# First modulation: silu(c) as the weight and the modulation matrix moving, in four column quarters

## The chip, the core and the metric

The kernel runs on one NeuronCore of a Trainium2 chip. Its engines are TensorE (PE, with its weight loads listed as PEld), VectorE (DVE), ScalarE (ACT), GpSimd (POOL) and SyncE (SP), which issues the DMAs. The metric is the device time of one execution in microseconds, the median of the runs.

## The reference, cut to what matters

Two transformer blocks of two layers each are computed for 512 tokens of width 1024, all in float32. Each layer of the first block scales and shifts its normalised input by vectors that depend on a condition `c`:

```python
def adaln_params(c, w, b):
    m = jax.nn.silu(c) @ w + b
    return [t[:, None, :] for t in jnp.split(m, 6, axis=-1)]
...
        sh1, sc1, g1, sh2, sc2, g2 = adaln_params(c, ada_w[layer], ada_b[layer])
        h = rms_norm(x, norm_mix_g[layer]) * (1.0 + sc1) + sh1
        if layer % 2 == 0:
            xr, gr, q, k, v = jnp.split(h @ ev_w_in[e], N_EVEN_SPLITS, axis=-1)
```

The change concerns `sh1` and `sc1` of layer 0: 2 x 1024 numbers, each a sum over 1024 products, needed before the first projection can start.

## The kernel before

Features lie on the 128 partitions, so a 1024-wide vector is 8 chunks of 128, and activations are stored as chunks of 128 x 512 tokens. Projections run three float32r matmuls for each product (high x high, high x low, low x high parts), 512 columns each in the startup.

The startup is `layer0_in`. It spawns eight tasks `first_chunk(c)`. Each loads 1 MB of the modulation matrix (two tiles `raw` of 128 x 4 x 256 floats: for 8 k chunks the 128 columns of the shift and the 128 of the scale that belong to chunk c), multiplies it with `silu_c`, adds the bias on DVE (tile `mod`), makes the scale column (`A`), and from that the chunk of h: `t` on DVE, the high part on ACT, the low part on DVE. Beside them `first_w(k)` loads a strip of 128 x 768 projection weights, whose high part ACT casts and whose low part DVE forms. `xnorm_all` sums squares of x, has PE spread the sum over the partitions by the matrix `ones`, and forms `rstd` on ACT and DVE. The main task then runs, for each of the 8 chunks k, six banks of three matmuls: 144 matmuls of 128x512, that end in six PSUM banks. ACT copies these out, and the attention and recurrence of layer 0 begin.

All engines execute their own queue in order. The order is fixed when the program is built: `Flow` runs the tasks with estimated costs, and each engine takes the ready operation of the best priority. A changed cost or a new operation can therefore move other operations. The other modulation vectors (layer 0 segments 2 to 5 and layer 1) are made in the background by DVE (`ada_half`: one step for each k chunk, 140 steps of the form `t<-a,silu_c,t`), folded into the tile `adap`, and turned by small PE matmuls against `sel`.

In `first_chunk` before, a 128x128 block of the matrix is the weight and one column of `silu_c` moves: 16 matmuls for a chunk, each with one output column. A float32 matmul appears in the trace as two records. PE's matmuls are all written in a helper, so they share line 304.

Of the kernel before, what the change touches and what calls it, by code (L numbers as in the profile page):

```python
# [13 lines left out]
ALU = mybir.AluOpType  # L14
AX = mybir.AxisListType

P = 128
S = 512
D = 1024
KC = 8  # L20
# [36 lines left out]
LAT = 0.15  # L57
# [33 lines left out]
class Flow:  # L91
# [18 lines left out]
    def put(s, name, n=1):  # L110
        s.free[name] += n
        still = []
        for t, k, spare in s.waiting[name]:
            if s.free[name] >= k + spare:
                s.free[name] -= k
                s.at(s.now, s.step, t, None)
            else:
                still.append((t, k, spare))
        s.waiting[name] = still
# [89 lines left out]
def body(ctx, tc, I, out, upto=8):  # L209
    nc = tc.nc  # L210
    T, V, A, G = nc.tensor, nc.vector, nc.scalar, nc.gpsimd
# [11 lines left out]
    ev, spawn, put = fl.event, fl.spawn, fl.put  # L223
# [4 lines left out]
    def mk(pool, shape, dt=F32, tag=None):  # L228
        cnt[0] += 1
        return pools[pool].tile(list(shape), dt, tag=tag or pool, name=f"{pool}{cnt[0]}", bufs=BUFS.get(tag))  # L230

    def big(dt=F32, shape=(P, 2, S)):
        return mk("a", shape, dt)

    def tmp(n=S):
        return mk("t", (P, n))
# [4 lines left out]
    def bank():  # L241
        cnt[0] += 1
        return psp.tile([P, S], F32, tag="b", name=f"b{cnt[0]}")

    def const(name, shape, dt=F32):
        return cp.tile(list(shape), dt, tag=name, name=name)


    def size(ap):
        n = 1  # L250
        for d in ap.shape[1:]:
            n *= d
        return n

    def ve(n, fast=False):
        return (0.52 if fast else 1.04) * n * 1e-3 + 0.07
# [4 lines left out]
    def tt(o, a, b, op, prio=None):  # L261
        return Op("V", ve(size(o)), lambda: V.tensor_tensor(o, a, b, op), prio=prio)  # L262

    def stt(o, a, sc, b, op0, op1, prio=None):
        return Op("V", ve(size(o)) + ptr(sc), lambda: V.scalar_tensor_tensor(o, a, sc, b, op0, op1), prio=prio)  # L265
# [6 lines left out]
    def vcopy(o, a, fast=True):  # L272
        return Op("V", ve(size(o), fast), lambda: V.tensor_copy(o, a))  # L273
# [11 lines left out]
    def act(o, a, f, bias=None, scale=1.0, accum=None, prio=None):  # L285
        kw = {}
        if bias is not None:
            kw["bias"] = bias
        if accum is not None:
            kw["accum_out"] = accum  # L290
        c = 0.83e-3 * size(o) + 0.07 + 0.09 * (not isinstance(scale, float)) + 0.09 * (accum is not None) + 0.12 * (bias is not None)
        return Op("A", c, lambda: A.activation(o, a, f, scale=scale, **kw), tab=SET_OF.get(f.name), prio=prio)  # L292

    def acopy(o, a):
        return Op("A", 0.83e-3 * size(o) + 0.07, lambda: A.copy(o, a))  # L295
# [4 lines left out]
    def mm(cost, *args, lat=0.0):  # L300

        def go():
            for o, l, r, st, sp in args:
                T.matmul(o, l, r, start=st, stop=sp)  # L304
        return Op("T", cost, go, lat=lat)
# [11 lines left out]
    def f4(n):  # L317

        return n / 600 + 0.0133
# [8 lines left out]
    vec = const("vec", (P, NVEC))  # L328
# [8 lines left out]
    sel4 = const("sel4", (P, 4, P))  # L337
    eps = const("eps", (P, 1))
    silu_c = const("silu_c", (P, 8))
    adap = const("adap", (P, 192))  # L340
    mods = [const(f"mod{l}", (P, 48)) for l in range(2)]
    acol = {k: const("A%d%d" % k, (P, 8)) for k in ((0, 1), (0, 4), (1, 1), (1, 4))}

    def vv(name, j=None):
        o, w = VEC[name]
        return vec[:, o : o + w] if j is None else vec[:, o + j : o + j + 1]
# [598 lines left out]
    def setup():  # L945
        G.memset(ones, 1.0 / D)
        G.memset(eps, EPS)
        yield Op("D", 0.3, lambda: nc.sync.dma_start(vec, I["vec"]), lat=2.2)
        yield act(silu_c, vv("c"), AF.Silu)

    const_done, decay_done = ev(), []

# [47 lines left out]
    def first_chunk(c, x, ready, nd, loaded):  # L1000

        raw = [big(shape=(P, 4, 256)) for _ in range(2)]
        yield [Op("D", 1.45, lambda i=i: nc.sync.dma_start(raw[i], I["ada0"][c, i]), lat=2.2) for i in range(2)]
        loaded.set()
        yield ready
        yield ("pt", 1)
        ps = bank()
        yield mm(16 * 0.111, *[(ps[:, i : i + 1], raw[k // 4][:, k % 4, i * P : i * P + P], silu_c[:, k : k + 1], k == 0, k == KC - 1)
                               for i in range(2) for k in range(KC)], lat=LAT)
        put("a", 2)  # L1010
        sh, sc = mods[0][:, c : c + 1], mods[0][:, 8 + c : 9 + c]
        o = VEC["ada_b0"][0]
        yield [tt(sh, ps[:, 0:1], vec[:, o + c : o + c + 1], ALU.add), tt(sc, ps[:, 1:2], vec[:, o + 8 + c : o + 9 + c], ALU.add)]
        put("pt")
        a = acol[0, 1][:, c : c + 1]
        yield stt(a, sc, 1.0, vv("gm0", c), ALU.add, ALU.mult)
        yield ("t", 1)
        t = tmp()
        for e in nd:
            yield e  # L1020
        yield stt(t, xs[c], a, rstd, ALU.mult, ALU.mult)
        yield act(x.h(c), t, AF.Identity, bias=sh)
        yield stt(x.l(c), t, sh, x.h(c).bitcast(F32), ALU.add, ALU.subtract)
        put("t")
        for hf in range(2):
            x.ready[c][hf].set()
# [9 lines left out]
    def layer0_in():  # L1036
# [3 lines left out]
        def after(e, gen):  # L1040
            yield e
            yield from gen

        ready = spawn(setup(), P_CRIT)

        def load_x(i):
# [15 lines left out]
        def chunks():  # L1062
            prev = []
            for c in range(KC):
                yield ("a", 2)
                prev.append(spawn(first_chunk(c, x, ready, nd, loaded[c]), P_CRIT))
                yield ("fw", 1)
                yield ("a", 3)
                fw[c] = (big(F32R, (P, 768)), big(F32R, (P, 768)))
                spawn(first_w(c, fw[c], fr[c]), P_CRIT)  # L1070
            yield loaded[CC]
            spawn(consts(), P_CRIT)
            yield loaded[KC - 1]
            spawn(weights(), P_W)
            for d in prev:
                yield d
# [931 lines left out]
```

## Time and profile before

| | us |
|---|---|
| median of 3 runs | 2870.63 |
| lowest, highest | 2869.69, 2872.17 |
| the profiled execution | 2870.89 |
| its span in the trace | 2869.1 |
| PE busy in it | 2789.7 (97%) |
| DVE busy | 1809.6 (63%) |
| ACT busy | 1257.5 (44%) |

Times of a view count from the start of the span; 1.8 us of the execution lie outside it. A busy PE is not a PE at its peak: the granted clock and the kind of matmul say what a busy microsecond does. In the views of the trace, the time in square brackets at the end of a row is the idle time of the engine ahead of it and what ended it.

### The profile page before, as it was taken

How to read it: one execution, taken by the hardware profiler on the slowest of the kernel's cores; microseconds unless marked ns; L12 is line 12 of the kernel's file. 1: busy time of each engine (PE TensorE's matmuls, PEld its weight loads, DVE VectorE, ACT ScalarE, POOL GpSimd, SP SyncE). 2: the span in 40 equal slices, each digit the busy share in tenths (PEclk: the TensorE clock that was granted, in tenths of full speed). 3: DMA queues.
4: the chain of work that ended last, by engine and by line, in shares of the span. 5: the costliest groups of instructions: out<-in, count | busy, mean ns of one | idle time of the engine just before them, and what ended most of it. 6: DMA issues, size and time to landing. Idle time of an engine off the chain costs nothing.

```text
span 2869.1 us, 44005 instructions
## 1 busy us (share of the span) xinstructions
PE 2789.7 (97%) x17374; PEld 2483.8 (87%) x17374; DVE 1809.6 (63%) x4137; ACT 1257.5 (44%) x2733; POOL 5.0 (0%) x54
## 2 busy tenths in 40 slices
PE   8998999999999999999989999989999999899999
PEld 7886987888988888898979888889899999788888
DVE  3798997447677444588794333666766767853333
ACT  2674432324654322256553322455655554442221
POOL 0000000000000000000000000000000000000000
PEclk8998999999999999999999999999999999999999
DMA  6444366232122232321222223221121122213321
GB/s 249 142 159 172 118 207 218 88 103 74 60 67 82 88 105 93 105 88 45 68 88 74 93 99 103 97 66 62 58 71 66 56 75 89 74 60 103 102 97 66
DMA packets 80271, 281.91 MB, mean 98 GB/s; under 512 B 8896, under 2 KB 11712, under 8 KB 80064
## 3 DMA queue, kind: packets, MB, share of 16 engines
q1 hardware_dynamic: 80064, 279.10, 28.6%
q8 instruction: 136, 2.23, 0.3%
q14 instruction: 71, 0.58, 0.1%
HBM read 276.97 MB, written 2.10 MB: 97 GB/s over the span
## 4 chain that ended last, share of the span: by engine, by line
PE 90%; DVE 6%; issue 1%; ACT 1%; DMA 1%; SPq 0%; DVEq 0%; ACTq 0%
PE b L304 86%; PE b L310 4%; DVE t L262 1%; DVE t L265 1%; DVE a L262 1%; DMA a<-in_ada_dram 1%; DVE x L262 1%; DVE x L265 1%; DVE a L265 0%; ACT t L292 0%; ACT a L295 0%; DVE a L1141 0%; ACT a L292 0%; DVE s L276 0%; DVE s L262 0%
## 5 line engine op out<-in xcount | busy, mean ns | idle before, releaser
L304 PE MATMUL b<-a,a 128*128 128x256 f32 (+4 forms) x15024 | 2560.3, 333 | 21.3 <-DVE a L262 8.1
L304 PEld LDWEIGHTS b<-a,a 128*128 128x128 f32 (+1 forms) x15024 | 2211.5, 191 | 294.5 <-issue 24.3
L295 ACT CAST a<-a 128x1024 fp32r<-128x1024 f32 (+1 forms) x354 | 357.4, 1034 | 319.8 <-DVE a L262 199.7
L262 DVE TENSOR_TENSOR a<-a,a 128x1024 fp32r<-128x1024 f32 (+2 forms) x362 | 428.4, 1195 | 8.3 <-ACT a L295 6.3
L292 ACT ACTIVATE t<-b 128x512 f32<-128x512 f32 x150 | 88.8, 597 | 345.6 <-PE b L304 344.6
L262 DVE TENSOR_TENSOR x<-b,x 128x512 f32<-128x512 f32 (+1 forms) x144 | 81.5, 571 | 206.6 <-PE b L304 206.1
L295 ACT COPY t<-b 128x512 f32<-128x512 f32 (+3 forms) x186 | 98.0, 529 | 195.8 <-PE b L304 123.9
L265 DVE SCALAR_TENSOR_TENSOR x<-b,mod,x 128x256 f32<-128x256 f32 (+1 forms) x176 | 104.7, 602 | 111.7 <-PE b L304 110.6
L295 ACT COPY a<-b 128x512 f32<-128x512 f32 (+2 forms) x178 | 85.1, 480 | 180.8 <-PE b L304 116.9
L273 DVE CAST a<-t 128x512 fp32r<-128x512 f32 x64 | 27.3, 426 | 203.6 <-ACT t L292 203.6
L265 DVE SCALAR_TENSOR_TENSOR a<-a,vec,a 128x256 fp32r<-128x256 f32 x288 | 132.4, 479 | 34.8 <-ACT a L292 34.2
L310 PE MATMUL b<-ident,t 128*128 128x128 f32 x832 | 131.1, 280 | 19.5 <-DVE t L262 12.0
L304 PEld LDWEIGHTS b<-a,t 128*128 128x128 f32 x1024 | 128.6, 197 | 12.4 <-ACT t L295 4.5
L304 PE MATMUL b<-a,t 128*128 128x64 f32 (+1 forms) x1024 | 135.2, 279 | 2.4 <-ACT t L295 2.3
L292 ACT ACTIVATE a<-a,vec 128x256 fp32r<-128x256 f32 x288 | 132.3, 500 | 1.0 <-DMA a<-in_kvw_dram 0.9
L310 PEld LDWEIGHTS b<-ident,t 128*128 128x128 f32 x832 | 97.9, 144 | 37.3 <-DVE t L262 15.1
L292 ACT ACTIVATE t<-t,s,s 128x256 f32<-128x256 f32 (+3 forms) x192 | 113.4, 593 | 23.4 <-DVE s L265 23.2
L292 ACT ACTIVATE t<-t 128x512 f32<-128x512 f32 x108 | 67.6, 633 | 122.9 <-DVE t L265 121.1
L262 DVE TENSOR_TENSOR t<-t,t 128x256 f32<-128x256 f32 (+5 forms) x201 | 104.6, 523 | 18.2 <-ACT t L292 16.9
L262 DVE TENSOR_TENSOR a<-t,a 128x512 fp32r<-128x512 f32 (+1 forms) x188 | 107.6, 596 | 4.0 <-ACT a L295 0.7
L276 DVE TENSOR_REDUCE s<-t 128x8 f32<-128x512 f32 (+1 forms) x84 | 56.4, 672 | 80.8 <-ACT t L292 80.6
L265 DVE SCALAR_TENSOR_TENSOR t<-a,silu_c,t 128x512 f32<-128x512 f32 x140 | 104.4, 746 | 1.4
(101 smaller groups left out, 1461.7 us busy)
## 6 DMA issues: line engine op xcount, KB each, us to landing
a<-in_ada_dram SPq DMA_DIRECT2D x96, 512.0 KB, 4.5
a<-in_gu_dram SPq DMA_DIRECT2D x88, 512.0 KB, 4.3
a<-in_mu_dram SPq DMA_DIRECT2D x64, 512.0 KB, 4.1
a<-in_md_dram SPq DMA_DIRECT2D x64, 512.0 KB, 3.7
a<-in_kvw_dram SPq DMA_DIRECT2D x48, 512.0 KB, 4.1
a<-in_dn_dram SPq DMA_DIRECT2D x44, 512.0 KB, 3.8
a<-in_aqkv_dram SPq DMA_DIRECT2D x24, 512.0 KB, 4.2
a<-in_bwq_dram SPq DMA_DIRECT2D x24, 512.0 KB, 3.7
```

Of the source, the lines that this page charges most:

```text
L262: return Op("V", ve(size(o)), lambda: V.tensor_tensor(o, a, b, op), prio=prio)
L265: return Op("V", ve(size(o)) + ptr(sc), lambda: V.scalar_tensor_tensor(o, a, sc, b, op0, op1), prio=prio)
L273: return Op("V", ve(size(o), fast), lambda: V.tensor_copy(o, a))
L276: return Op("V", ve(size(a)), lambda: V.tensor_reduce(o, a, AX.X, ALU.add))
L292: return Op("A", c, lambda: A.activation(o, a, f, scale=scale, **kw), tab=SET_OF.get(f.name), prio=prio)
L295: return Op("A", 0.83e-3 * size(o) + 0.07, lambda: A.copy(o, a))
L304: T.matmul(o, l, r, start=st, stop=sp)
L310: T.transpose(o, a, ident)
```

## The change

`silu(c)` becomes the weight. It is stored as `silu32`, 8 blocks of 128x32 of which only the first column is not zero. For each k chunk, 256 columns of the matrix (128 of the shift, 128 of the scale) move through a 32-column quarter of the array, quarter k % 4, into partitions 32 (k % 4) and following of a bank; two k chunks share a quarter and accumulate. The eight matmuls leave four partial sums in rows 0, 32, 64 and 96, and zeros in the other rows. ACT copies the 128x256 block to SBUF, and two matmuls with a column of ones (`one1`) sum over the partitions and turn the rows into the two columns that DVE reads as before.

```diff
+    silu32 = const("silu32", (P, 8, 32))
+    one1 = const("one1", (P, 1))
...
+        G.memset(one1, 1.0)
+        G.memset(silu32, 0.0)
...
+        yield vcopy(silu32[:, :, 0:1], silu_c.unsqueeze(2))
...
         ps = bank()
-        yield mm(16 * 0.111, *[(ps[:, i : i + 1], raw[k // 4][:, k % 4, i * P : i * P + P], silu_c[:, k : k + 1], k == 0, k == KC - 1)
-                               for i in range(2) for k in range(KC)], lat=LAT)
+        part = lambda i: ps[i * 32 : i * 32 + 32, :256]
+
+        yield mm(4 * f4(256) / 2 + 0.1, *[(part(k % 4), silu32[:, k, :], raw[k // 4][:, k % 4, :], k < 4, k > 3) for k in range(KC)], lat=LAT)
         put("a", 2)
+        yield ("t", 1)
+        rows = tmp(256)
+        yield acopy(rows, ps[:, :256])
+        yield mm(2 * 0.222, *[(ps[:, 256 + i : 257 + i], rows[:, i * P : i * P + P], one1, True, True) for i in range(2)], lat=LAT)
+        put("t")
...
-        yield [tt(sh, ps[:, 0:1], vec[:, o + c : o + c + 1], ALU.add), tt(sc, ps[:, 1:2], vec[:, o + 8 + c : o + 9 + c], ALU.add)]
+        yield [tt(sh, ps[:, 256:257], vec[:, o + c : o + c + 1], ALU.add), tt(sc, ps[:, 257:258], vec[:, o + 8 + c : o + 9 + c], ALU.add)]
```

On PE, from the norm's matmul (`t,ones`) to the first projection matmuls (`a,a 128x512`), the order before is this; `silu_c` marks the modulation's one-column matmuls of chunks 1 and 2:

```order
L304 MATMUL b_200<-t_120,ones 128x512
L304 MATMUL b_224<-silu_c,a_132 128x1 x4
L304 MATMUL b_224<-silu_c,a_133 128x1 x4
L304 MATMUL b_224<-silu_c,a_132 128x1 x4
L304 MATMUL b_224<-silu_c,a_133 128x1 x4
L304 MATMUL b_262<-silu_c,a_135 128x1 x4
L304 MATMUL b_262<-silu_c,a_136 128x1 x4
L304 MATMUL b_262<-silu_c,a_135 128x1 x4
L304 MATMUL b_262<-silu_c,a_136 128x1 x4
L304 MATMUL b_111<-a_103,a_123 128x512
```

The same place on PE after the change; `32x256` are the quarter matmuls, `one` the turning ones, and tile numbers differ between the two programs:

```order
L304 MATMUL b_197<-t_124,ones 128x512
L304 MATMUL b_186<-one_89,t_203 128x1 x2
L304 MATMUL b_227<-a_136,silu_88 32x256 x4
L304 MATMUL b_227<-a_137,silu_88 32x256 x4
L304 MATMUL b_227<-one_89,t_241 128x1 x2
L304 MATMUL b_257<-a_139,silu_88 32x256 x4
L304 MATMUL b_257<-a_140,silu_88 32x256 x4
L304 MATMUL b_113<-a_105,a_127 128x512
L304 MATMUL b_113<-a_106,a_127 128x512
L304 MATMUL b_113<-a_105,a_128 128x512
L304 MATMUL b_114<-a_105,a_127 128x512
L304 MATMUL b_114<-a_106,a_127 128x512
```

Sixteen rows of one column become eight of 256, and the two turning matmuls of a chunk stand behind other work: chunk 0's behind the norm's matmul, chunk 2's behind six projection matmuls.

On ACT before, between the cast of the first weight strip and the first two chunks of h:

```order
L295 CAST a_123<-a_131 128x768
L292 ACTIVATE t_121<-b_200,eps 128x512
L292 ACTIVATE rstd<-t_121 128x512
L292 ACTIVATE t_121<-rstd 128x512
L295 CAST a_125<-a_134 128x768
L292 ACTIVATE a_103<-t_218,mod_89 128x512
```

On ACT after, the same place, where each COPY of 128x256 is a new operation that waits for the quarter matmuls of its chunk:

```order
L295 CAST a_127<-a_135 128x768
L295 COPY t_203<-b_186 128x256
L292 ACTIVATE t_125<-b_197,eps 128x512
L292 ACTIVATE rstd<-t_125 128x512
L292 ACTIVATE t_125<-rstd 128x512
L295 CAST a_129<-a_138 128x768
L295 COPY t_241<-b_227 128x256
L292 ACTIVATE a_105<-t_222,mod_91 128x512
```

The copy of chunk 0 has moved in ahead of the norm's first operation, and that of chunk 1 ahead of the first chunk of h.

## Rows read from the trace of the kernel before

**Rows 1.** The page, part 4: shares of the chain that ended last.
```profile
PE 90%; DVE 6%; issue 1%; ACT 1%; DMA 1%; SPq 0%; DVEq 0%; ACTq 0%
```
**Rows 2.** Timeline of PE, 0 to 98 us: start, us, engine, line, operation, xcount.
```profile
11.94 6.96 PE L304 MATMUL b<-silu_c,a 128*128 128x1 f32 x32 [11.94 <-DMA a<-in_ada_dram]
18.76 2.06 PE L304 MATMUL b<-t,ones 128*128 128x512 f32 x2
20.61 13.65 PE L304 MATMUL b<-silu_c,a 128*128 128x1 f32 x64
34.12 4.00 PE L304 MATMUL b<-a,a 128*128 128x512 f32 x9
37.95 3.90 PE L304 MATMUL b<-silu_c,a 128*128 128x1 f32 x32
...
52.00 4.25 PE L304 MATMUL b<-silu_c,a 128*128 128x1 f32 x32
...
60.11 6.82 PE L304 MATMUL b<-silu_c,a 128*128 128x1 f32 x32
...
81.04 3.63 PE L304 MATMUL b<-silu_c,a 128*128 128x1 f32 x32
84.53 25.72 PE L304 MATMUL b<-a,a 128*128 128x512 f32 x143
```
**Rows 3.** Windows of PE: stretch, its length, PE busy (records), PEclk, DMA share, GB/s.
```profile
10.00:20.00 10.00, 8.06 (x34) 1.00 1.03 416
...
38.00:54.00 16.00, 16.00 (x91) 0.89 0.34 108
54.00:72.00 18.00, 18.00 (x69) 0.53 0.47 153
72.00:84.00 12.00, 12.00 (x85) 1.00 0.28 95
...
480.00:500.00 20.00, 20.00 (x90) 1.00 0.32 106
```
**Rows 4.** Timeline of DVE in the startup: the norm's sum, its last steps.
```profile
13.05 0.69 DVE L262 TENSOR_TENSOR t<-t,t 128x512 f32<-128x512 f32 x1
...
23.68 0.43 DVE L270 TENSOR_SCALAR t<-t 128x512 f32<-128x512 f32 x1
27.47 0.23 DVE L262 TENSOR_TENSOR mod<-b,vec 128x1 f32<-128x1 f32 x2 [3.36 <-PE b L304]
...
28.48 0.69 DVE L262 TENSOR_TENSOR rstd<-rstd,t 128x512 f32<-128x512 f32 x1
```
**Rows 5.** Timeline of ACT: a weight cast, the norm's first step, the first bank copy.
```profile
14.04 0.83 ACT L295 CAST a<-a 128x768 fp32r<-128x768 f32 x1 [1.22 <-DMA a<-in_evfirst_dram]
...
20.91 0.69 ACT L292 ACTIVATE t<-b,eps 128x512 f32<-128x512 f32 x1 [6.05 <-PE b L304]
...
94.62 1.27 ACT L295 COPY t<-b 128x512 f32<-128x512 f32 x2 [4.16 <-PE b L304]
```
**Rows 6.** Timeline of PE: float32 matmuls on 64 rows, at the low clock.
```profile
259.38 2.08 PE L304 MATMUL b<-a,a 64*128 64x384 f32 x4
...
272.53 2.07 PE L304 MATMUL b<-a,a 64*128 64x512 f32 x2
```
**Rows 7.** Groups of ACT by form: busy, mean ns of one, idle before.
```profile
L295 ACT COPY t<-b 128x256 f32<-128x256 f32 x16 | 6.0, 375 | 6.1 <-PE b L310 6.0
```
**Rows 8.** Timeline of SP's queue: the last strip of first weights.
```profile
45.38 0.33 SPq L1030 DMA_DIRECT2D a<-in_evfirst_dram  x1
```
**Rows 9.** Groups of DVE, 97 to 320 us: the background modulation.
```profile
L265 DVE SCALAR_TENSOR_TENSOR t<-a,silu_c,t 128x512 f32<-128x512 f32 x65 | 48.3, 742 | 0.4
```
**Rows 10.** Windows of all engines: PE, PEld, DVE, ACT, POOL busy, PEclk, DMA share, GB/s.
```profile
240.00:260.00 20.00, 15.06 (x72) 10.67 (x72) 19.85 (x42) 9.84 (x26) 0.00 (x0) 0.82 0.78 271
...
360.00:380.00 20.00, 20.00 (x94) 16.66 (x93) 19.90 (x32) 6.02 (x9) 0.20 (x2) 1.00 0.71 240
```
**Rows 11.** Waits of PE: for whom, us in total, times, longest.
```profile
PE b L304 <- DVE adap L276: 2.6, 1, 2.6
```

## The prediction, made before the changed kernel ran

> **What bounds the kernel now.** I read the page first: the chain that ended last lies on PE for 90% of the span [rows 1]. So only what PE executes, or waits for, can move the end. The change touches the start alone, so I then read PE in order of time up to 98 us [rows 2], beside windows of the same stretch [rows 3].
>
> Three things stand there. PE does nothing for 11.94 us, until the first modulation data land; then chunk 0's 32 one-column records take 6.96 us, and the next 64 take 13.65 us, which is 0.213 us each [rows 2]. The first projection matmul starts only at 34.12 us. Later chunks take 3.6 to 6.8 us each.
>
> Second, DMA is saturated only early: 416 GB/s from 10 to 20 us, 108 from 38 to 54 [rows 3]. By then PE is the bound, not the data.
>
> Third, the clock. From 60.11 to 66.79 us, in a stretch granted 0.53 on average, a one-column record also takes 0.213 us, and at a granted 1.00 (72 to 84 us) 3.63/32 = 0.113 us [rows 2, 3]. So 0.213 is the price at 1.2 GHz, 0.113 at 2.4 GHz. From 12 to 34 us PE pays 0.213 too: it ran at the lower level although that row reads 1.00, presumably because no clock record exists so early. The level was low while PE worked through one-column matmuls, rose after 9 projection matmuls (34.12 to 37.95), and fell again after chunks 3 to 5 [rows 2, 3]. One-column matmuls seem not to hold the clock up.
>
> **Where the startup ends before.** After chunk 7's last record (about 84.6 us) 51 of the 144 wide projection matmuls are left. ACT's first copy of a finished bank starts at 94.62 us [rows 5]; five banks of three matmuls follow it, so PE leaves the startup near 97.6 us. One 128x512 matmul at full clock: 20.00 us over 90 records is 0.222 [rows 3]; a few per cent of records are missing, and 512 columns at 2.4 GHz are 0.213, so I take 0.216, and 0.43 at the low level.
>
> **The change, part by part.** Per chunk it removes 32 records whose time is weight loading (3.6 us at full clock, 6.8 at the low one). It adds 8 float32 matmuls of 256 columns (32-column weights, four quarters in turn), an ACT copy of 128x256, and 2 one-column matmuls (4 records) that turn the row into columns.
>
> (a) The eight matmuls. Two records of 128x512 with the same float32 rate take 2.06 us at the low clock [rows 2]; with the 0.35 us tail of the last one taken off, a record of 512 columns is 0.85 us, so one of 256 columns is 0.43 low and 0.213 full. Sixteen records in line are 3.4 us full, 6.8 us low, exactly what is removed. Everything hangs on whether the quarters run side by side. No row shows column quarters. The nearest are float32 matmuls on the two row halves of the array: at the low clock, two records of one matmul take 2.07 us, and four records of a pair, one of the same size and one of three quarters of it, take 2.08 us [rows 6]. Halves overlap fully. I take the same for quarters: two rounds of two records, 0.85 us full, 0.9 with the hand-over, 1.7 low. Bounds: 0.9 to 3.5 us.
>
> The Trainium skill, page "TensorE: Matmul & The Clock Gate", section "The mechanism" of its Part 3, says that a weight load overlaps matmuls in flight only if its row group differs. Column quarters share all rows, so by that rule the quarters would serialise, which speaks against this change and gives the first rival's time; the same part also reports 2.38 times for three column tiles. No run so far shows which holds here.
>
> (b) The two turning matmuls: 4 x 0.113 = 0.45 us full, 0.9 low.
>
> (c) The round trip PE, ACT, PE. The copy costs 0.37 us [rows 7], plus the matmul tail of 0.17 and two hand-overs of about 0.1: 0.75 us. From chunk 3 on the order puts three projection matmuls (0.65 us) between the quarters and the turn, which covers it unless ACT is in a weight cast of 0.82 us [rows 5]. I take 0.4 us of stall per chunk; ends 0 and 0.9. So a late chunk costs 0.9 + 0.45 + 0.4 = 1.75 us against 3.6 to 6.8.
>
> (d) Start of the projection. Chunk 0's second half lands 0.52 MB/416 GB/s = 1.26 us after 11.94, so its quarters end near 14.2. The sum of squares is ready at 13.05 + 0.69 = 13.74 us [rows 4], so the norm's matmul can run from 14.2 to 16.3, where before it waited behind chunk 0 until 18.76. The norm's rest, without waits between, is 3.9 us (20.91 to 24.11 plus a 0.69 multiply; before, DVE stood waiting for chunk 1 at 27.47 and the multiply came at 28.48) [rows 4, 5]: rstd at 20.3. DVE then does a cast remainder 0.95, chunk 0's scale 0.75, five tiny steps 0.85, chunk 1's scale 0.75 and the low part 0.75: 24.3 us. Chunk 2's data land at 13.2 + 2 x 3.47 (1.44 MB per chunk) = 20.1 and its quarters are done by 22. So the projection starts at 24 us, against 34.12.
>
> (e) From there PE bounds: 144 x 0.216 = 31.1 us; first 4 to 7 us at the low clock, 2.6 us lost (1.7 to 6); chunk 2's turn 0.5; chunks 3 to 7, 5 x 1.75 = 8.8. End at 24.3 + 31.1 + 2.6 + 0.5 + 8.8 = 67.3 us. Data for chunk 7 land by 38 us, long before.
>
> Before, the same part took 97.6 - 34.1 = 63.5 us: 31.1 of projection, 22.2 of chunks 3 to 7 (3.90, 4.25, 6.82 and twice 3.63) [rows 2], about 10 of low clock. The difference is 30.3 us: 10 from the earlier start, 13 from the chunks, 7 from the clock.
>
> (f) What costs nothing: two fills on POOL, idle then, and one DVE copy of 128x8 near 3.5 us, 8 us ahead of its first reader. DMA: the first 26 issues keep their order, and where SP waits for a freed buffer (the last weight strip is issued at 45.38 [rows 8]), the buffer comes earlier. The next weights queue behind on SP and land by 45 us, ahead of 67; gone that cover, a 1 to 3 us gap.
>
> (g) After the startup. Per engine the order of operations is the same except up to PE row 2,100 (about 500 us). In it the background modulation (140 DVE steps of 0.74 us [rows 9]) shifts: 58 instead of 72 of them stand ahead of layer 0's last residual, so 14 x 0.742 = 10.4 us of DVE work moves from the attention stage into the first feed-forward. In the attention tail, 240 to 260 us, PE is busy only 15.06 us of 20 with DVE at 19.85 [rows 10], so that helps a little. In the feed-forward PE once waits 2.6 us for that background work [rows 11], and this may grow. I count both at zero, 7 us either way.
>
> **Sum.** The profiled execution takes 2870.89 us (span 2869.1, 1.8 outside it), the same as the median of 2870.63. 2870.9 - 30.3 = 2840.6, so 2841 us.
>
> **Rivals.**
> 1. The quarters don't run side by side, so the change doesn't do what it says. A chunk costs 3.5 us full. Chunk 0 ends at 17 to 19, the projection starts at 27 to 34, and chunks 3 to 7 cost 5 x 4.3 = 21: end of startup between 80 and 89, gain 8 to 18, 2853 to 2863, middle 2857. For it: no row of column tiles. Against: the row halves.
> 2. The gain is partly given back behind the startup. PE arrives 30 us earlier, but DVE, busy 19.90 us of 20 from 360 to 380 [rows 10], has the same background work plus 10.4 us; in-order PE then waits at the six small matmuls that read it. At 10 to 20 us given back, 2851 to 2861, middle 2855. For it: the 2.6 us wait. Against: that work has no reader near.
> 3. The clock stays low, because narrow quarters count as little as one-column matmuls did. Then 144 x 0.43 = 62 us, chunks 5 x 3 = 15, start 25: end near 102, 4 us later than before, 2875: no gain. If the quarters also serialise: start 36, 62 for the projection, chunks 5 x 8.2 = 41: end at 139, 2912. This is the side that is slower; it decides once nearly all of the startup runs at 1.2 GHz. Against: 9 wide matmuls raised the clock before, and here 18 stand together.
> 4. The attention tail also tightens with less DVE work ahead: 8 us more, 2831.
>
> **How the numbers follow.** Forecast 0.60 (own range 2833 to 2850), rival 1 0.17, rival 2 0.09, rival 3 0.04 (side by side) and 0.05 (in line), rival 4 0.05. The range 2831 to 2858 takes the forecast, rival 4 in half and most of 1 and 2. Within 0.2% (5.7 us), about what a measurement of this kernel can tell from no change, lies rival 3's first case: 0.04. Slower is its second: 0.05. Faster is the rest, 0.91.
>
> **What would show it.** In the new trace: eight quarter matmuls within 0.9 to 1.7 us (right) or 3.4 and more (rival 1); the norm's matmul near 14 us; the first projection matmul near 24; the granted clock at 1.00 from about 30 us on (else rival 3); the first bank copy near 64; PE's idle time at 240 to 320 us and waits on the adap tile no longer than before (else rival 2). A projection start after 30 us, or a startup end after 75, would make the forecast wrong.

## The result, and the profile after the change

The changed kernel takes 2846.05 us (median of 4 runs, 2841.89 to 2848.08) against 2870.16 us for the kernel before on the same chip. The ratio is 0.9914 with an interval of 0.9896 to 0.9931, a gain of 24.1 us. The profiled execution has a span of 2846.1 us.

The page of the kernel after, parts 1 and 4: busy time by engine, and the shares of the chain that ended last.

```profile
PE 2765.8 (97%) x17278; PEld 2448.6 (86%) x17278; DVE 1808.4 (64%) x4138; ACT 1257.1 (44%) x2738; POOL 6.1 (0%) x56
...
PE 90%; DVE 6%; ACT 1%; issue 1%; DMA 1%; SPq 0%; DVEq 0%; ACTq 0%
```

PE is busy for 23.9 us less than before, and the chain still lies on it for 90% [rows 1]. So the time went where the prediction looked for it, on PE.

The timeline of PE after the change, startup (start, us, engine, line, operation, xcount, idle time before in brackets); it answers to [rows 2].

```profile
11.86 2.27 PE L304 MATMUL b<-a,silu 128*32 128x256 f32 x16 [11.86 <-DVE s L269]
14.06 2.08 PE L304 MATMUL b<-t,ones 128*128 128x512 f32 x2
...
19.29 0.61 PE L304 MATMUL b<-one,t 128*128 128x1 f32 x4 [0.76 <-ACT t L295]
...
22.49 0.80 PE L304 MATMUL b<-a,a 128*128 128x512 f32 x1 [1.60 <-ACT a L292]
23.52 2.50 PE L304 MATMUL b<-a,a 128*128 128x512 f32 x5 [0.23 <-DVE a L265]
25.81 0.85 PE L304 MATMUL b<-one,t 128*128 128x1 f32 x4
...
29.01 1.07 PE L304 MATMUL b<-a,silu 128*32 128x256 f32 x16
30.01 0.96 PE L304 MATMUL b<-a,a 128*128 128x512 f32 x3
30.80 0.50 PE L304 MATMUL b<-one,t 128*128 128x1 f32 x4
31.16 7.77 PE L304 MATMUL b<-a,a 128*128 128x512 f32 x33
```

A chunk's 16 records of quarter matmuls take 1.07 us at full clock. The next group starts 1.00 us after the first of them, and the group behind the turning matmuls starts 0.36 us after those. PE waits for ACT's copy once, for 0.76 us, ahead of chunk 1's turn at 19.29 us. Behind 23.52 us no row of the startup has a bracket, so from there on PE waits for no copy.

The timeline of ACT after the change: its first bank copy, which answers to the last row of [rows 5].

```profile
64.22 0.59 ACT L295 COPY t<-b 128x512 f32<-128x512 f32 x1 [2.08 <-PE b L304]
```

It stood at 94.62 us before, so the startup ends 30.4 us earlier. At the end of the program only 23.0 us of that are left in this execution. The start of some operations in both traces and in those of five experiments of the next section (us; "residual" is the DVE operation that adds a PSUM bank into x, of which there are 320):

| | before | after | after, again | old order | dearer steps | warm | warm and dearer |
|---|---|---|---|---|---|---|---|
| first bank copy | 94.6 | 64.2 | 63.7 | 64.8 | 63.8 | 60.9 | 61.5 |
| residual 1 | 219.8 | 195.4 | 191.6 | 190.0 | 185.4 | 192.3 | 183.0 |
| residual 49 | 425.2 | 400.1 | 396.3 | 396.2 | 395.1 | 396.9 | 391.8 |
| residual 57 | 562.1 | 539.3 | 532.5 | 532.8 | 527.5 | 536.2 | 524.2 |
| last residual | 2865.8 | 2842.8 | 2835.2 | 2836.7 | 2831.5 | 2839.7 | 2828.4 |

From residual 57 on every column runs in step with before, within 1 us. What was given back was given back in the first 560 us. The windows of PE after the change there (stretch, length, PE busy and records, granted clock, DMA share, GB/s):

```profile
127.00:134.00 7.00, 7.00 (x35) 0.54 0.76 249
472.00:479.00 7.00, 6.67 (x20) 0.52 0.26 80
```

Nearly all of both stretches ran at the lower clock level (1.2 GHz). About 7 us at half speed are an estimated 3.5 us lost, twice. The timeline of PE after the change shows what came just ahead:

```profile
126.37 0.30 PE L310 MATMUL b<-ident,t 128*128 128x128 f32 x1 [2.05 <-DVE t L262]
...
472.33 1.89 PE L304 MATMUL b<-adap,sel 128*128 128x16 f32 x8 [2.06 <-DVE adap L276]
```

Each time PE had waited 2 us for DVE, and the clock fell. The kernel before has such a place too: PE's one wait for `adap` there, with the granted clock just behind it (a row of its timeline, then a window of PE).

```profile
472.93 1.06 PE L304 MATMUL b<-adap,sel 128*128 128x16 f32 x8 [2.60 <-DVE adap L276]
...
474.60:478.10 3.50, 3.50 (x10) 0.51 0.09 35
```

Its low stretch there is half as long. The longest low stretches lie in the attention tail and just behind it, and add up to 37.5 us in both kernels (252.8 to 263.0, 269.8 to 290.3 and 314.2 to 321.0 us before; 229.9 to 264.0 and 291.3 to 294.8 us after), so they do not tell the two apart.

### The profile page after: what moved, and what is told of

Same layout as the page of the kernel before. It is cut to its first block, busy times and chain, and to the rows that moved or that the text cites. A ratio compares the mean times of both kernels' runs of the same rounds, so it can differ in the third digit from the quotient of the medians.

```text
span 2846.1 us, 43812 instructions
## 1 busy us (share of the span) xinstructions
PE 2765.8 (97%) x17278; PEld 2448.6 (86%) x17278; DVE 1808.4 (64%) x4138; ACT 1257.1 (44%) x2738; POOL 6.1 (0%) x56
## 4 chain that ended last, share of the span: by engine, by line
PE 90%; DVE 6%; ACT 1%; issue 1%; DMA 1%; SPq 0%; DVEq 0%; ACTq 0%
PE b L304 86%; PE b L310 4%; DVE t L265 1%; DVE t L262 1%; DVE a L262 1%; DMA a<-in_ada_dram 1%; DVE x L262 1%; DVE x L265 0%; DVE a L265 0%; ACT t L292 0%; ACT a L295 0%; ACT a L292 0%; DVE a L1152 0%; ACT L220 0%; DVE s L276 0%
## 5 line engine op out<-in xcount | busy, mean ns | idle before, releaser
L295 ACT CAST a<-a 128x1024 fp32r<-128x1024 f32 (+2 forms) x354 | 357.5, 1034 | 325.1 <-DVE a L262 199.7
L310 PEld LDWEIGHTS b<-ident,t 128*128 128x128 f32 x832 | 98.4, 145 | 30.4 <-DVE t L262 13.4
L262 DVE TENSOR_TENSOR t<-t,t 128x256 f32<-128x256 f32 (+5 forms) x201 | 104.3, 522 | 14.1 <-ACT t L292 12.7
```

Source lines behind the costliest of these rows:

```text
L310: T.transpose(o, a, ident)
```

## Experiments

The question left by the result is in two parts: what the 30 us at the start consist of, and why some of them are lost later. The kernel before, run beside them, took 2870.06 us for one quarter, the 128 columns, the repeat and the old order; 2869.5 for two quarters, both kernels with filling matmuls, and the background costs; and 2870.94 for both edits together.

**One quarter for all k chunks.** The eight matmuls of a chunk all use quarter 0, in line, and only that quarter's 32 rows are copied and turned.

```diff
-        yield mm(..., *[(part(k % 4), silu32[:, k, :], raw[k // 4][:, k % 4, :], k < 4, k > 3) ...
+        yield mm(..., *[(part(0), silu32[:, k, :], raw[k // 4][:, k % 4, :], k == 0, k == KC - 1) ...
...
-        yield acopy(rows, ps[:, :256])
+        yield acopy(rows[0:32, :], ps[0:32, :256])
-        yield mm(2 * 0.222, *[(..., rows[:, i * P : i * P + P], one1, True, True) ...
+        yield mm(2 * 0.222, *[(..., rows[0:32, i * P : i * P + P], one1[0:32, :], True, True) ...
```

> The changed kernel with all eight k chunks in the first column quarter, so nothing can run side by side; planned costs and so the order of every engine are kept (the copy and the turn touch 32 partitions instead of 128). Theory (quarters side by side carry the gain): a chunk's sixteen records take 3.4 us at full clock instead of 1.0, the startup's first bank copy comes at 76 to 86 us instead of 64.2, and the time is 2858 to 2868 us. Rival (data or the round trip over ACT set the startup): the bank copy stays below 68 us and the time within 4 us of the changed kernel.

Measured: 2859.04 us (2857.96 to 2860.45), ratio 0.9963 [0.9949, 0.9977]. Rows of PE's timeline, then of ACT's, of this kernel:

```profile
44.37 3.64 PE L304 MATMUL b<-a,silu 128*32 128x256 f32 x16
...
81.07 0.59 ACT L295 COPY t<-b 128x512 f32<-128x512 f32 x1 [2.18 <-PE b L304]
```

In line a chunk takes 3.64 us, with quarters 1.07. The first bank copy is 16.9 us later than after the change, and the median 13 to 16 us later than the two of the changed kernel. So the quarters do run side by side and are worth more than half of the gain. Without them the change would still gain 11 us, though its chunks are no shorter than the 3.63 us of before [rows 2].

**Two quarters** (`part(k % 2)`, with 64 rows copied and turned) give the point between.

> The changed kernel with the eight k chunks in two column quarters instead of four, order kept. Theory (quarters run side by side as many as there are): at full clock a chunk's sixteen records take 1.8 to 2.0 us, between 1.07 with four and 3.64 with one, and the first bank copy comes near 69 us (64.2 with four, 81.1 with one). Rival (two already hide everything else): the bank copy at 64 to 65 us.

Measured: 2846.67 us in one run. Rows of PE and ACT of this kernel:

```profile
38.98 1.92 PE L304 MATMUL b<-a,silu 128*32 128x256 f32 x16
...
68.74 0.59 ACT L295 COPY t<-b 128x512 f32<-128x512 f32 x1 [2.14 <-PE b L304]
```

3.64, 1.92 and 1.07 us for one, two and four quarters: the time falls almost with their number, and the first bank copy comes at 81.07, 68.74 and 64.22 us, as the theory had it.

**The kernel before with 128 equal columns moving.** The weights stay the blocks of the matrix, and the column of `silu_c` is repeated 128 times as the moving side. It computes the same numbers, at the same price in weight loads: the change without its idea, but with wide matmuls.

```diff
-        yield mm(16 * 0.111, *[(ps[:, i : i + 1], raw[...][...], silu_c[:, k : k + 1], k == 0, k == KC - 1) ...
+        yield mm(16 * 0.111, *[(ps[:, i * P : i * P + P], raw[...][...], silu_c[:, k : k + 1].to_broadcast([P, P]), k == 0, k == KC - 1) ...
...
-        yield [..., tt(sc, ps[:, 1:2], ...)]
+        yield [..., tt(sc, ps[:, P : P + 1], ...)]
```

> The kernel before with one edit: silu(c) moves as 128 equal columns instead of one, so a record still takes the time of its weight load (0.113 us at full clock) but the array has columns in it all the time. Theory (in the startup the clock is low because one-column matmuls do not hold it up, worth about 7 us): granted clock at 1.00 through most of 20 to 98 us, first bank copy at 84 to 90 us instead of 94.6, time 2860 to 2866 us. Rival (the clock there has another reason): bank copy at 93 to 96 us and 2868 to 2872 us.

Measured: 2848.89 us (2846.64 to 2850.45), ratio 0.9928 [0.9913, 0.9942]: more than either theory gave. The timeline of PE of this kernel, and ACT's first bank copy:

```profile
19.05 7.31 PE L304 MATMUL b<-silu_c,a 128*128 128x128 f32 x64
26.20 0.50 PE L304 MATMUL b<-a,a 128*128 128x512 f32 x1
...
28.93 3.73 PE L304 MATMUL b<-silu_c,a 128*128 128x128 f32 x32
32.42 9.13 PE L304 MATMUL b<-a,a 128*128 128x512 f32 x39
...
74.41 1.27 ACT L295 COPY t<-b 128x512 f32<-128x512 f32 x2 [2.45 <-PE b L304]
```

The windows of PE of the same kernel (columns as above):

```profile
20.00:40.00 20.00, 19.71 (x131) 1.00 1.01 394
40.00:60.00 20.00, 20.00 (x138) 1.00 0.58 195
60.00:80.00 20.00, 20.00 (x115) 1.00 0.41 145
```

Chunk 3 is followed 3.49 us after its start (28.93 to 32.42), as chunk 7 was before at full clock (81.04 to 84.53 [rows 2]). Nothing got cheaper but the clock: 1.00 in all three windows, where before it was 0.89 and 0.53 [rows 3]. The 64 records of chunks 1 and 2 take 7.31 us instead of 13.65. The first bank copy moves by 20.2 us, and the shift stays at 20 us to the end. So 20 of the 30 us of the start are the price of letting the clock fall. With the one-quarter kernel the first bank copy gives the whole sum in three steps: 94.62 to 74.41 for the clock (20.2 us gained), 74.41 to 81.07 for the new form in line, with its turns and at an equal clock from 30 us on (6.7 lost), and 81.07 to 64.22 for the four quarters (16.9 gained). The last two together are the other 10 us. The shares hold in this order of steps: the one-quarter kernel, whose clock reads 1.00 from 20 us on but which lacks the quarters, leaves the startup 13.5 us earlier than before.

**The kernel before, with the clock raised ahead of it.** 32 matmuls of `ones` with `ones` run while PE would wait for the first data; `ones` is filled earlier for them.

```diff
     def setup():
-        G.memset(ones, 1.0 / D)
...
+        G.memset(ones, 1.0 / D)
         ready = spawn(setup(), P_CRIT)
...
+        yield mm(0.01, *[(pss[0][:, :P], ones, ones, True, True) for _ in range(32)])
```

> The kernel before with the same 32 matmuls of ones while PE waits for the first data, and nothing else. It tells apart why the clock was low until 37.7 us. Theory (one-column matmuls let it fall): the clock is up at 12 us, and falls during the chunks 0 to 2, so that late records of the 64 cost 0.21 us again; first bank copy at 89 to 94 us. Rival (the clock was low only because PE had stood still until 12 us): chunks 0 to 2 at 0.113 us a record throughout, first bank copy at 80 to 86 us.

Measured: 2870.51 us in one run, so nothing was gained; the first bank copy comes at 95.55 us, 0.9 us later than before and not at 89 to 94. The windows of PE of this kernel, and one row of its timeline:

```profile
0.00:10.00 10.00, 9.02 (x56) 1.00 0.79 262
10.00:20.00 10.00, 9.05 (x47) 0.67 1.03 416
20.00:40.00 20.00, 20.00 (x98) 0.57 0.83 334
```
```profile
19.69 13.65 PE L304 MATMUL b<-silu_c,a 128*128 128x1 f32 x64
```

The records of the clock have it rise at 6.7 us and fall at 13.5, while PE worked through the one-column matmuls of chunk 0; the next 64 cost the same 13.65 us as before. A wait of 0.83 us for the data stands ahead of chunk 0 here and may have had a part in the fall. It does not account for the level staying low until 37.4 us, with PE busy for 20.00 of 20 us. With the 128-column experiment this settles it: a stream of one-column matmuls, which shows as a busy PE, ran at the lower level even when the level was high as it began.

**The changed kernel again, and with the old order behind the startup.** The first has no edit. The second one tells the planner the costs of before for the new operations, which puts the background modulation back where it stood.

```diff
-        yield mm(4 * f4(256) / 2 + 0.1, *[(part(k % 4), ...
+        yield mm(16 * 0.111, *[(part(k % 4), ...
-        yield acopy(rows, ps[:, :256])
-        yield mm(2 * 0.222, *[...], lat=LAT)
+        yield Op("A", 0.0, lambda: A.copy(rows, ps[:, :256]), lat=0.0)
+        yield mm(0.0, *[...], lat=0.0)
```

> The changed kernel again, beside the three others on the same chip. Expected 2842 to 2848 us, first bank copy at 64 us, with the place where the 7 us go visible again: if the low clock between 220 and 300 us falls in another place than in the first profile, the order alone does not set it.

> The changed kernel, its work untouched, but with the planner told that a chunk costs what it did before (1.776 us on PE, nothing for the copy and the turn), so that after the startup every engine has the order of the kernel before. The changed kernel leaves the startup 30 us earlier and ends 23 us earlier. Theory A (the new order of the attention stage loses the 7 us): the first bank copy stays near 64 us and the time is 2838 to 2841 us. Theory B (work of DVE and low clock behind the startup lose it whatever the order): 2843 to 2849 us.

Measured: the changed kernel 2843.24 us (2840.31 to 2846.58), ratio 0.9909 [0.9894, 0.9924]; with the old order 2842.83 us (2841.99 to 2844.76), ratio 0.9908 [0.9893, 0.9923]. The second lies between the bands of its theories, 0.2 us from theory B's. The two medians are 0.4 us apart, so the moved background work (14 steps, 10.4 us of DVE by the prediction) costs nothing that can be measured in the median. The profiled execution of the repeat kept its whole gain (last residual 30.6 us earlier). Its PE timeline and windows at the two places:

```profile
125.35 0.30 PE L310 MATMUL b<-ident,t 128*128 128x128 f32 x1 [1.52 <-DVE t L262]
...
468.78 1.06 PE L304 MATMUL b<-adap,sel 128*128 128x16 f32 x8 [1.69 <-DVE adap L276]
```
```profile
120.00:136.00 16.00, 14.45 (x106) 1.00 0.59 211
456.00:476.00 20.00, 18.31 (x85) 1.00 0.33 110
```

The same program waits 1.52 and 1.69 us here instead of 2.05 and 2.06, the clock stays up, and the end comes 7.6 us earlier. The low stretch between 220 and 300 us that the expectation asks about is in both executions, at 225.6 to 259.8 us here and 229.9 to 264.0 in the first, so it is not the difference. The 7.6 us are as much as the spread of the changed kernel, 2840.3 to 2848.1 us over both sets of 4 runs. That the longer runs among them all had these low stretches is argued, since only two of the eight were profiled. Nor does the length of a wait alone settle whether the clock falls: in the one-quarter kernel it fell behind a shorter wait (a row of its PE timeline, then a window of PE).

```profile
142.76 0.30 PE L310 MATMUL b<-ident,t 128*128 128x128 f32 x1 [1.59 <-DVE t L262]
...
143.40:150.20 6.80, 6.80 (x32) 0.50 0.65 229
```

**Filling matmuls in the changed kernel.** The clock is low there from 21.7 to 28.5 us, and by the times of the matmuls also ahead of its first record at 18.3 us. 32 matmuls of `ones` fill the wait for the first data, 3 and 6 more the gaps after chunks 1 and 2.

```diff
-        G.memset(ones, 1.0 / D)
...
+    def idle_work(n):
+        yield mm(0.01, *[(fill[0][:, :P], ones, ones, True, True) for _ in range(n)])
...
+        if c in (1, 2):
+            spawn(idle_work(3 * c), -1)
...
+        G.memset(ones, 1.0 / D)
         ready = spawn(setup(), P_CRIT)
...
+        yield mm(0.01, *[(pss[0][:, :P], ones, ones, True, True) for _ in range(32)])
```

> The changed kernel with idle work for PE: 32 matmuls of 128x128 ones while it waits for the first data, 3 more after chunk 1 and 6 after chunk 2, in waits that the trace of the changed kernel shows; the order of everything else is kept. Theory (what is left of the low clock, up to 28.5 us, costs 3 to 5 us): granted clock at 1.00 from before 12 us, first bank copy at 59 to 62 us instead of 63.7 to 64.2, time 2838 to 2841 us. Rival (until 23 us the data and the chain over DVE set the start, so the clock there is hidden): the first projection matmul still at 22 to 23 us and the bank copy no earlier than 62.5.

Measured: 2843.84 us (2840.68 to 2845.44), ratio 0.9906 [0.9893, 0.992]: no better than the changed kernel. Rows of its PE and ACT timelines, and its windows of PE:

```profile
20.87 1.60 PE L304 MATMUL b<-ones 128*128 128x128 f32 x12
22.23 1.64 PE L304 MATMUL b<-a,a 128*128 128x512 f32 x6
...
20.64 0.72 ACT L292 ACTIVATE a<-t,mod 128x512 fp32r<-128x512 f32 x1 [1.84 <-DVE t L265]
...
60.87 0.59 ACT L295 COPY t<-b 128x512 f32<-128x512 f32 x1 [2.08 <-PE b L304]
```
```profile
124.00:131.00 7.00, 7.00 (x34) 0.52 0.76 257
469.00:476.00 7.00, 6.59 (x20) 0.51 0.26 84
```

The projection starts hardly earlier (22.23 against 22.49), but not because its input is late: ACT has the high part of h ready at 21.36 us, 1.1 us earlier than in the changed kernel, and PE is then in the last filling matmuls, which give way at 22.23. The startup ends 3 us earlier, the price of the low clock at its beginning: from the first projection matmul to chunk 3's quarters PE takes 3.4 us (22.23 to 25.64) instead of 6.5. The time still misses the theory's 2838 to 2841. This execution had both low stretches behind the startup, and at residual 57 it was behind the repeat of the changed kernel (536.2 against 532.5).

**The planner told what the background steps cost.** Their durations in the trace are 0.75, 0.48, 0.71 and 0.68 us, where the planner counts 0.66, 0.40, 0.60 and 0.60. With the measured costs the operations that read them are put later.

```diff
+    def dear(op, c):
+        op.cost = c
+        return op
...
-                yield ts(acc, raw, silu_c[:, 0:1], None, ALU.mult)
+                yield dear(ts(acc, raw, silu_c[:, 0:1], None, ALU.mult), 0.48)
...
-                yield stt(acc, raw, silu_c[:, k : k + 1], acc, ALU.mult, ALU.add, prio=P_ADA)
+                yield dear(stt(acc, raw, silu_c[:, k : k + 1], acc, ALU.mult, ALU.add, prio=P_ADA), 0.75)
...
-        yield Op("V", 0.6, lambda: V.transpose(w, acc))
-        yield red(adap[:, o : o + 16], ...)
+        yield Op("V", 0.71, lambda: V.transpose(w, acc))
+        yield dear(red(adap[:, o : o + 16], ...), 0.68)
```

> The changed kernel with the planner told what the background modulation's DVE steps take in the trace (0.75, 0.48, 0.71 and 0.68 us instead of 0.66, 0.40, 0.60 and 0.60), so that PE's small matmuls that read adap stand later in its queue; the startup is untouched. Theory (a part of the 7 us lost behind the startup in the first profile is PE waiting for that background work, and the clock that falls after it): no wait on adap over 1 us and no low clock between 300 and 480 us, time 2838 to 2842 us. Rival (that loss changes from run to run and has little to do with where the small matmuls stand): 2841 to 2847 us as without the edit.

Measured: 2836.28 us (2832.75 to 2838.25), ratio 0.9881 [0.9867, 0.9894], 7 to 10 us below the two medians of the changed kernel, and below both kernels. A row of PE's timeline, and its windows, of this kernel:

```profile
477.41 0.96 PE L304 MATMUL b<-adap,sel 128*128 128x16 f32 x8
```
```profile
120.00:136.00 16.00, 16.00 (x124) 1.00 0.46 167
460.00:480.00 20.00, 20.00 (x94) 1.00 0.41 140
```

PE reads `adap` without waiting, its wait near 125 us is gone too, and the clock stays at 1.00 at both places. By the table above it gains 3.8 us on the repeat between residuals 49 and 57, where the repeat's PE waits 3.3 us for `adap` in all, and 6.8 us on the first execution of the changed kernel, whose clock fell there as well. The edit also reorders the attention stage (6.2 us ahead of the repeat at residual 1, 1.2 at residual 49), so not all of it is the waits.

**Both edits together.**

> The two edits together: the 32 + 9 filling matmuls over a tile of ones that brought the first bank copy from 63.7 to 60.9 us (e5), and the planner's dearer background steps, with which PE waited for no modulation vector and no stretch from 290 to 672 us had a low clock (e8, 2836.3 us). Theory: what the first edit gained at the start was lost again only through low stretches of the clock behind waits of PE that the second edit takes away, so the 3 us of the start are added to e8's: 2831 to 2835, first bank copy near 60.9, no low stretch between 290 and 672 us. Rival: the waits of the first layer (PE waits for the vector L262 near 125 us, which neither edit removes) take the gain of the start again, as in e5: 2835 to 2839, and the shift against the kernel before, -33 at the first scan, is -31 or less by 200 us.

Measured: 2834.27 us (2832.58 to 2837.62), ratio 0.9876 [0.986, 0.9893]. ACT's first bank copy, and the windows of PE, of this kernel:

```profile
61.49 0.59 ACT L295 COPY t<-b 128x512 f32<-128x512 f32 x1 [2.08 <-PE b L304]
```
```profile
120.00:136.00 16.00, 16.00 (x125) 1.00 0.44 157
290.00:672.00 382.00, 378.36 (x1937) 1.00 0.43 149
```

The median lies in the theory's band, but the interval of the ratio overlaps that of the edit before, so the medians alone do not settle it. The traces do for the profiled executions: 2.3 us ahead of the dearer steps alone at the first bank copy, and 3.1 us ahead at the last residual. In this pair, where PE waits at neither place, the gain of the start is kept. The wait near 125 us on which the rival counted is in neither trace. This is the fastest version measured.

## Why the prediction was right, and where its steps were off

The time was forecast at 2841 us, with 2831 to 2858. 2846.05 lies in that range and in the forecast's own (2833 to 2850), and it is faster. Of the rivals the second came nearest: a part of the gain was given back, though about 5 us and not 10 to 20.

**(a) The quarters** were the open question, and the row halves [rows 6] were the right rows to go by: 1.00 us from the chunk's start to the next group against 0.9 forecast. The Trainium skill, page "TensorE: Matmul & The Clock Gate", section "The mechanism", says that a weight load overlaps matmuls in flight only if the row group differs, and by that rule the quarters would have taken turns. The traces do not agree: four quarters with all rows in common took 1.07 us, one quarter 3.64, which is 3.4 times as fast. The 2.38 times that the Trainium skill gives on the same page, section "Measured speedup vs the span model", is for three column tiles. The records show what runs side by side: the first matmul records of the four quarters of chunk 3 start at 29.006, 29.013, 29.019 and 29.026 us, while in the one-quarter kernel one record starts 0.216 us after the other.

**(b) and (c)** The turn was forecast at 0.45 us and takes 0.50, or 0.36 to the next group. The stall for ACT's copy, taken at 0.4 us, is zero for the late chunks: the projection matmuls between (three, for chunk 4 six) cover it. A late chunk costs 1.36 us, not 1.75.

**(d) The projection's start** was forecast at 24 us and came at 22.49. The norm's matmul at 14.06 and the quarters' end at 14.1 us were forecast to 0.2 us. `rstd` is complete in DVE's timeline after the change at 20.15 us, 20.3 forecast:

```profile
19.46 0.69 DVE L262 TENSOR_TENSOR rstd<-rstd,t 128x512 f32<-128x512 f32 x1
...
22.72 0.75 DVE L265 SCALAR_TENSOR_TENSOR a<-t,mod,a 128x512 fp32r<-128x512 f32 x1
```

And in ACT's:

```profile
21.72 0.72 ACT L292 ACTIVATE a<-t,mod 128x512 fp32r<-128x512 f32 x1 [2.48 <-DVE t L265]
```

The 1.5 us too many lie behind it. DVE's steps to the low part of h end at 23.47 us, 24.3 forecast, and the first projection matmul does not take that part: it takes the high part, which ACT had ready at 22.44. For the low part PE then waits 0.23 us ahead of 23.52.

**(e) The end of the startup** was forecast with the first bank copy near 64, and it is 64.22. The total of 30.3 us was exact (30.4), which is in part luck, since its terms are off by up to 3.6 us and the errors cancel. The earlier start is 34.12 - 22.49 = 11.6 us (10 forecast). Chunks 3 to 7 are 22.2 - 5 x 1.36 = 15.4 us (13 forecast). The rest, 3.4 us, was forecast at 7 and called the clock. **The step that failed is this last name.** The prediction saw that one-column matmuls seemed not to hold the clock up, but booked only the low clock of the projection matmuls under it. The 128-column experiment measures 20 us for the clock: 34.12 - 26.20 = 7.9 us of the earlier start, 3.8 us of chunks 3 to 5 (3.90, 4.25 and 6.82 us where 3.73 is the price at full clock), and the remaining 8.5 us in the rest of the startup, which is wide matmuls and two chunks at full clock. The prediction itself had the rows for it: 0.213 against 0.113 us a record for chunks 0 to 2 [rows 2]. So the total came out by place, while the cause behind two thirds of it stood in a term of 7. The quarters, on which the prediction hung everything, are worth the 16.9 us that the one-quarter kernel lacks.

**(f)** held: no gap of PE in the startup behind 23.52 us.

**(g) What happens behind the startup** was counted at zero with 7 us either way. Measured: 7.4 us given back in one execution (30.4 to 23.0), next to nothing in the other (30.9 to 30.6). Over all 8 runs of the changed kernel the median is 2844.8 us, so of 30.4 us some 5 are lost on the way. The mechanism named in rival 2 was half right: PE does wait for `adap`, as it did before [rows 11], but in sum only 0.5 and 0.7 us longer (3.1 and 3.3 us in the two profiled executions against 2.6). What sets the two executions apart is that the clock falls behind a wait in one of them, which no step of the prediction held. That this is what the median loses is argued, not shown. The moved background work, which it feared, is not the cause: with the old order the median is the same.

**Rivals.** Rival 1 (quarters in line) was priced at 2857 and measured, as the one-quarter kernel, at 2859.04. Rival 3 (the clock stays low) did not come: the window from 30 to 40 us after the change reads 1.00. Rival 4 (a tighter tail) did not come with the change, but the dearer planner costs gave a tighter attention stage for a while: 6.2 us ahead of the repeat at residual 1, of which 1.2 were left at residual 49.

The windows of PE after the change, which answer to [rows 3]:

```profile
20.00:30.00 10.00, 8.18 (x48) 0.66 1.03 406
30.00:40.00 10.00, 10.00 (x61) 1.00 1.03 402
```

What stays open: why the two waits differ by about 0.5 us between executions of the same program, why the clock falls behind one wait of 1.6 us and not behind another of 1.7, and how the gain of the dearer steps divides between the reordered attention stage and the waits.

## What to carry to other kernels

Make a matrix-vector product on TensorE with the vector as a narrow weight and the matrix moving, and spread the k chunks over the four column quarters; one copy and two small matmuls bring the row back to columns. Where one-column matmuls stand in a stream, compare the time of a record with its time in a window of full granted clock: a busy PE can be at half speed, and moving more columns at the same weight price, even useless ones, can be worth more than removing work. A gain at the start can be lost again where PE waits later and the clock falls behind the wait, so look there for work with slack that the planner counts too cheap, and give it the measured cost.

## What was not expected of the hardware

- One-column matmuls with 128x128 weights do not hold the clock: raised to 1.00 ahead of them, it fell at 13.5 us in the middle of chunk 0, stayed low until 37.4 us under a busy PE, and 64 records took 13.65 us. With 128 columns each, 64 records took 7.31.
- Column quarters overlap almost fully for float32 matmuls with all 128 rows: 3.64, 1.92 and 1.07 us with one, two and four quarters.
- The granted clock reads 1.00 in a view ahead of the clock's first record (at 37.7 us before the change), although the time of the matmuls there is that of the lower level: 0.213 us a record from 20.61 us on [rows 2].
- Two executions of the same program had waits of 2.05 and 2.06 us followed by some 7 us at the lower level, and waits of 1.52 and 1.69 us with the clock at 1.00 behind them. Their ends lie 7.6 us apart.
